# One layer of a gMLP / RG-LRU / HGRN2 encoder on one core: branch generators cut into smaller steps, gate sigmoids moved to the merge phase, one bank emptied by ScalarE

## The chip, the cores and the metric

The kernel runs on one NeuronCore of a Trainium2 chip. Its engines are TensorE (PE; its weight loads are shown apart as PEld), VectorE (DVE), ScalarE (ACT), GpSimd (POOL) and SyncE (SP, used for DMA issue). The time is device microseconds of one execution. The kernel before takes 2251.32 us (median of 3 runs, 2247.9 to 2254.17).

## What is computed

One inference step of one layer for two request groups side by side, 512 new frames and 32 streaming frames (T = 544 columns), D = 2048:

```python
h  = rmsnorm(x, norm_g) * (1.0 + scale) + shift          # scale, shift, gate from silu(c) @ w_ada
z  = h @ w_in                                            # 2048 x 15360, 120 blocks of 128 columns
au, av, ag, lx, lg, hq, hf, hi, hg, mg = split(z)        # 8 blocks each, mg 48 blocks
ya = gelu(au) * (tril(ws) @ rmsnorm(gelu(av)) + bs) * silu(ag)              # gMLP
yb = rglru(causal_conv(lx)) * silu(lg)                                      # RG-LRU, a scan over time
yc = rmsnorm(hgrn2(silu(hq), hf, hi)) * onorm_g * silu(hg)                  # 8 heads, chunks of 64
ga, gb, gc = split(sigmoid(mg), 3)
out = (ga * (ya @ wb0) + gb * (yb @ wb1) + gc * (yc @ wb2)) @ w_out
y = rmsnorm(x + gate * out, final_g)
```

All is float32, with new states of the RG-LRU and HGRN2 branches as further outputs.

## The kernel before

Activations lie transposed: 128 features on the partitions, the 544 frames as columns, taken as two halves of HF = 272. Every large product is done with three matmuls per 128x128 weight tile: weights and activations are split into a rounded high part and a rest (`wh`, `wl`), and hi·hi, hi·lo and lo·hi are added in PSUM (`rows3`). ScalarE makes `wh` by a Copy, VectorE makes `wl` by a subtraction (`split`, called by `halved`, two tiles of 512 columns per weight half).

The first phase makes scale and shift. The second, the z phase, makes z = h @ w_in in 60 `Group`s of two 128-column blocks. A group is a 2x2 block product by a Strassen-like scheme with 7 products (numbers 1 to 7), each 8 weight tiles x 3 = 24 matmuls of 272 columns. Each product is an *item*: `prep` (the splits, and for products 7 and 6 a VectorE addition of two weight halves), `mul` (the 24 matmuls) and `after` (emptying of the PSUM bank). The order over groups is 2, 6, 1 of the next group, 5, 7 of the next group, 3, 4. Four banks (`pm`) are shared: products 1, 6, 5 and 3 add up in bank `a`, which ScalarE copies out after 1, 6, 5 and 3; product 2 has the bank `a2`, which the *next* group uses as its `a`, so that product 1 of the next group, two items later, needs it empty. VectorE empties bank `a2` at line 381 (it adds `u1`, the copy of product 1), and bank `c` at lines 390 and 395.

What is to be done with a group's two outputs stands in generators: `av_gen` and `gm_gen` (gMLP), `hg_gen` (one HGRN2 head), `lru_gen` (one block of the RG-LRU); `keep` post-processes and stores the outputs that are read later, in DRAM scratch. `pump()` advances every started generator by one step, up to its next `yield`; it is called once after each item. The head generators run one at a time, and every third call of `pump` leaves them out (`heads["tick"]`).

Nothing reorders the work: each engine executes its instructions in the order in which the Python code calls them. The main loop does, for item i: weight loads, `prep` of item i+2, `mul` of item i, `after` of item i, `pump`. So what a generator step calls on ScalarE stands between the emptying of bank i and the splits of item i+3. Adding DMAs (`load_adds`, line 266) are issued from GpSimd's queue.

The groups stand in `z_groups`: 4 of av, then 16 times a head group (hf/hq or hi/hg) and a *light* one (two blocks of mg), 3 light ones, 16 heavy ones (8 gMLP, 8 RG-LRU) with a light one after every fourth, and the rest of the light ones.

The third phase (`merge`) multiplies each branch output with its weight matrix in 48 blocks of 48 matmuls and scales each block by its gate, read back from scratch (`fetch`); the last (`out_items`) multiplies with w_out and normalizes.

Of the kernel before, what the change touches and what calls it, by code (L numbers as in the profile page):

```python
# [10 lines left out]
AF = mybir.ActivationFunctionType  # L11
# [95 lines left out]
def hybrid_step_kernel(ctx: ExitStack, tc: tile.TileContext, xT, cT, w_first, w_in, w_branch, w_out,  # L107
# [222 lines left out]
    class Group:  # L330
# [4 lines left out]
        def __init__(self, n, b1, b2, post, posts=None):  # L335
            self.n, self.b, self.post, self.posts = n, (b1, b2), post, posts or {}
            self.w, self.raw = {}, {}
# [4 lines left out]
        def add(self, i):  # L342
# [8 lines left out]
            elif i in (6, 4):  # L351
                n = self.q
            else:
                n = need({1: w_half(b1, 0), 2: w_half(b1, 1), 3: w_half(b2, 1), 5: w_half(b1, 0)}[i])
                if i == 5:
                    add(k - 5, n, w_half(b2, 0))
                else:
                    self.raw[i] = n

            def prep():  # L360
                assert not any(e[1] == n for e in adds)
                self.w[i] = halved(raws[n])
                if i in (7, 6):
                    m = self.raw[1 if i == 7 else 2]
                    tt(raws[n], raws[n], raws[m], op=OP.add)  # L365
                    done[m] = True
                elif i not in (1, 2):
                    done[n] = True

# [4 lines left out]
            def after():  # L374
# [76 lines left out]
    heads = {"next": 0, "ready": 0, "run": None, "tick": 0}  # L451

    def pump():
# [3 lines left out]
        heads["tick"] += 1  # L457
        if heads["tick"] % 3 == 0:
            return
# [169 lines left out]
    def av_gen(j, b):  # L629
        yield  # L630
# [29 lines left out]
    def gm_gen(g, cell):  # L660
# [23 lines left out]
        u, sg = cell["o"]  # L684
        a, s = px(), px()
# [44 lines left out]
    def hg_gen(h):  # L730
# [12 lines left out]
        t1, t2, g = hbuf(), hbuf(), zf  # L743
        act(t1.ap, zf.ap, AF.Abs)
        act(t2.ap, zf.ap, AF.Relu)
        ts(g.ap, zf.ap, 0.0, None, op0=OP.min)
        KO = qb.col - kb.col
# [734 lines left out]
```

## Time and profile before

| | |
|---|---|
| median of 3 runs | 2251.32 us |
| the profiled execution: its time, its span | 2244.99 us, 2243.3 us |
| PE busy in the span | 2052.4 us (91%) |
| DVE, ACT, POOL busy | 1292.6, 1138.4, 511.5 us (58%, 51%, 23%) |
| mean granted clock of PE | 0.953 |

The profile is one execution, taken by the hardware profiler. Times are us from the start of the span unless marked ns. "L381" is line 381 of the kernel; a line can be that of a helper (L190 is the call of every ScalarE activation, L232 the subtraction of every split, L324 every matmul of `rows3`). Names are the program's tile names: `pm` and `pp` are PSUM banks of the z phase and of the later phases, `px` small PSUM tiles of the generators, `arena` the pool of all SBUF buffers of the generators, `raw` and `q` loaded weights. In "x <- y" after a wait, y is the engine and line that ended it. PEclk is the granted share of TensorE's full clock: 1.00 is 2.4 GHz, 0.50 is 1.2 GHz.

### The profile page before, as it was taken

The numbers are of one execution on the slowest core, as the hardware profiler recorded it, in microseconds if no ns is written. First come the engines' busy times: TensorE is split into PE (matmuls) and PEld (weight loads), VectorE is DVE, ScalarE is ACT, GpSimd is POOL, SyncE is SP. The second block draws the span as 40 slices with busy tenths as digits, with TensorE's granted clock in tenths as the row PEclk, the third lists the DMA queues.
The fourth block names the chain that finished last, engine by engine and source line by source line (L and its number), as shares of the span: only waits on it lengthen the run. The fifth ranks groups of instructions, "written<-read, shape, count | busy, mean of one in ns | idle before, by whom it ended". The sixth has DMA issues, their size and how long they took to land.

```text
span 2243.3 us, 40766 instructions
## 1 busy us (share of the span) xinstructions
PE 2052.4 (91%) x15864; PEld 1944.7 (87%) x15864; DVE 1292.6 (58%) x2204; ACT 1138.4 (51%) x2163; POOL 511.5 (23%) x720
## 2 busy tenths in 40 slices
PE   5789979898999899899999999889998999999997
PEld 3279979898988888899899999888987999999996
DVE  3465557666656566557576676777775433442226
ACT  3456545656455566556565655466564322332223
POOL 0011123222223222323233132121122222220112
PEclk8689989999999989999999999999999999999998
DMA  7966656565556656566667776656665677665554
GB/s 308 365 189 181 191 150 192 157 183 166 146 165 165 176 156 185 144 171 174 175 187 202 174 209 175 166 144 166 154 164 187 221 197 184 195 199 182 172 170 165
DMA packets 135010, 412.23 MB, mean 184 GB/s; under 512 B 16128, under 2 KB 38432, under 8 KB 134816
## 3 DMA queue, kind: packets, MB, share of 16 engines
q1 hardware_dynamic: 87408, 261.08, 34.9%
q0 software_dynamic: 41424, 138.34, 27.0%
q10 hardware_dynamic: 5984, 10.19, 1.4%
q8 instruction: 125, 2.05, 0.4%
q14 instruction: 69, 0.57, 0.1%
HBM read 363.77 MB, written 45.78 MB: 183 GB/s over the span
## 4 chain that ended last, share of the span: by engine, by line
PE 55%; DVE 6%; issue 4%; ACT 3%; DMA 1%; POOL 1%; DVEq 0%; ACTq 0%; POOLq 0%
PE pm L324 29%; PE pp L324 22%; DVE wl L232 2%; ACT arena L190 1%; PE px L1067 1%; DVE q L365 1%; PE px L1263 1%; ACT wh L190 1%; PE px L814 1%; DVE arena L1052 0%; ACT L194 0%; DVE arena L381 0%; POOL arena L751 0%; DVE arena L395 0%; ACT L190 0%
## 5 line engine op out<-in xcount | busy, mean ns | idle before, releaser
L324 PE MATMUL pm<-x,wh 128*128 128x272 f32 x6720 | 1315.9, 295 | 76.3 <-DVE arena L381 29.8
L324 PEld LDWEIGHTS pm<-x,wh 128*128 128x128 f32 x6720 | 1087.2, 194 | 87.7 <-ACT wh L190 34.9
L324 PE MATMUL pm<-x,wl 128*128 128x272 f32 x3360 | 988.0, 294 | 5.2 <-DVE wl L232 4.8
L324 PEld LDWEIGHTS pm<-x,wl 128*128 128x128 f32 x3360 | 648.5, 193 | 9.5 <-DVE wl L232 9.4
L232 DVE TENSOR_TENSOR wl<-raw,wh 128x512 fp32r<-128x512 f32 x652 | 466.4, 742 | 303.1 <-ACT wh L190 301.9
L190 ACT ACTIVATE wh<-raw 128x512 fp32r<-128x512 f32 x652 | 387.9, 624 | 326.8 <-PE pp L324 174.8
L324 PE MATMUL pp<-x,wh 128*128 128x272 f32 x2560 | 485.9, 289 | 0.6 <-DVE arena L395 0.6
L324 PEld LDWEIGHTS pp<-x,wh 128*128 128x128 f32 x2560 | 401.2, 189 | 14.9 <-issue 14.3
L324 PE MATMUL pp<-x,wl 128*128 128x272 f32 x1280 | 369.0, 288 | 0.0
L232 DVE TENSOR_TENSOR wl<-q,wh 128x512 fp32r<-128x512 f32 x360 | 252.5, 721 | 199.4 <-ACT wh L190 196.9
L190 ACT ACTIVATE wh<-q 128x512 fp32r<-128x512 f32 x360 | 218.0, 624 | 121.2 <-PE pm L324 94.5
L190 ACT ACTIVATE arena<-arena 128x544 f32<-128x544 f32 (+5 forms) x310 | 160.7, 554 | 195.4 <-DVE arena L1316 76.8
L324 PEld LDWEIGHTS pp<-x,wl 128*128 128x128 f32 x1280 | 240.8, 188 | 0.2 <-DVE wl L232 0.2
L190 ACT ACTIVATE arena<-pm 128x272 f32<-128x272 f32 x240 | 94.0, 392 | 163.4 <-PE pm L324 143.1
L266 POOL DMA_DIRECT2D q<-in_w_in_dram x60 | 54.9, 915 | 483.8 <-DMA q<-in_w_in_dram 120.1
L365 DVE TENSOR_TENSOR q<-q,raw 128x1024 f32<-128x1024 f32 x120 | 148.5, 1238 | 4.1
L190 ACT ACT_TABLE_LOAD x72 | 92.4, 1283 | 54.8 <-DVE arena L1052 49.5
L266 POOL DMA_DIRECT2D raw<-in_w_in_dram x60 | 54.1, 902 | 213.5 <-DMA raw<-in_w_in_dram 89.6
L788 POOL TENSOR_TENSOR arena<-arena 128x544 f32<-128x544 f32 (+1 forms) x40 | 53.5, 1359 | 57.1 <-PE px L816 30.0
L1219 DVE TENSOR_TENSOR arena<-pp,arena 128x544 f32<-128x544 f32 x48 | 34.8, 724 | 41.8 <-PE pp L324 41.8
L190 ACT ACTIVATE arena<-px 128x128 f32<-128x128 f32 (+4 forms) x136 | 43.1, 332 | 24.6 <-PE px L897 13.8
L1326 POOL TENSOR_TENSOR tail<-tail,arena 128x544 f32<-128x544 f32 (+1 forms) x15 | 18.6, 1241 | 150.3 <-ACT arena L190 150.3
(265 smaller groups left out, 1467.1 us busy)
## 6 DMA issues: line engine op xcount, KB each, us to landing
raw<-in_w_in_dram SPq DMA_DIRECT2D x240, 512.0 KB, 4.9
q<-in_w_in_dram SPq DMA_DIRECT2D x60, 512.0 KB, 4.9
q<-in_w_in_dram POOLq DMA_DIRECT2D x60, 512.0 KB, 7.2
raw<-in_w_in_dram POOLq DMA_DIRECT2D x60, 512.0 KB, 6.5
raw<-in_w_branch_dram SPq DMA_DIRECT2D x48, 512.0 KB, 4.2
raw<-in_w_ss_dram SPq DMA_DIRECT2D x44, 512.0 KB, 7.1
raw<-in_w_out_dram SPq DMA_DIRECT2D x38, 512.0 KB, 4.7
raw<-in_w_gate_dram SPq DMA_DIRECT2D x32, 512.0 KB, 4.6
```

The source lines that it names most:

```text
L190: return nc.scalar.activation(out, in_, func, **kw)
L232: tt(lo, src, hi.bitcast(F32), op=OP.subtract)
L266: nc.gpsimd.dma_start(out=raws[n], in_=src, accum_op=OP.add)
L324: mm(p, a, rhs(k, r), start=start and i == 0 and q == 0, stop=stop and i == n - 1 and q == 2, **kw)
L365: tt(raws[n], raws[n], raws[m], op=OP.add)
L788: ptt(v, fv(src, 0, [[2 * m, nb], [m - 1, 2], [1, m]]), fv(src, m - 1, [[2 * m, nb], [0, 2], [0, m]]), op=OP.subtract)
L814: mm(fv(p, 64 * i, [[128, 2], [1, 64]]), x[:, 256 * i + 128:256 * i + 256], fv(x, 256 * i, [[256 + m, 2], [2 * m, nb], [1, m]]), start=Tru ...
L1067: mm(ri[n][h], w.ap[:, n * 128:(n + 1) * 128], xc.ap[:, h * HF:(h + 1) * HF], start=True, stop=True)
L1219: tt(two(g.ap), halves(p), two(g.ap), op=OP.mult)
L1263: mm(p[32 * i:32 * i + 2, :256], cs[:, 4 * q + i, :], w[:, i * 256:(i + 1) * 256], start=q == 0, stop=q == 3)
L1326: ptt(a[:, n], a[:, n], b.ap[:, n], op=OP.add)
```

## The change

Work that a generator did in one step is cut by further `yield`s, mostly so that a step has work of one kind of engine. `pump` advances the head generator at every call instead of two of three. The sigmoids of hq and hg become a generator of their own (`put_away`); the sigmoid of mg is left out there, and made in the merge phase on the gate that was read back. Bank `a2` is emptied by ScalarE, and `u1` is added later, in SBUF, with product 4. One light group more stands ahead of the heavy ones, and so one less after them. The rewriting of `prep` leaves its order as it was.

```diff
@@ class Group: after
                 elif i == 2:
                     self.o1 = buf()
-                    tt(self.o1.ap[:, :HF], banks[self.a2], self.u1.ap, op=OP.add)
-                    self.u1.free()
+                    act(self.o1.ap[:, :HF], banks[self.a2], AF.Copy)
...
                 elif i == 4:
+                    tt(self.o1.ap[:, :HF], self.o1.ap[:, :HF], self.u1.ap, op=OP.add)
                     tt(self.o1.ap[:, HF:], c, self.u2.ap, op=OP.add)
+                    self.u1.free()
@@ pump
-        heads["tick"] += 1
-        if heads["tick"] % 3 == 0:
-            return
@@ av_post, av_gen
-                act(o.ap, o.ap, AF.Gelu_apprx_tanh)
                 start(av_gen(j + i, o))
...
     def av_gen(j, b):
+        yield
+        act(b.ap, b.ap, AF.Gelu_apprx_tanh)
         yield
@@ gm_gen
         act(t1.ap, sg.ap, AF.Sigmoid)
+        yield
         tt(sg.ap, sg.ap, t1.ap, op=OP.mult)
         tt(sg.ap, sg.ap, u.ap, op=OP.mult)
+        yield
@@ hg_gen (28 yields in place of 18)
         act(t1.ap, t1.ap, AF.Exp, scale=-1.0)
         act(t1.ap, t1.ap, AF.Ln, bias=cv[:, 1:2])
+        yield
+        ts(g.ap, zf.ap, 0.0, None, op0=OP.min)
         ptt(g.ap, g.ap, t1.ap, op=OP.subtract)
         tt(t2.ap, t2.ap, t1.ap, op=OP.add)
+        yield
         act(kb.ap, t2.ap, AF.Exp, scale=-1.0, bias=ln1)
         ts(t1.ap, g.ap, -80.0, None, op0=OP.max)
+        yield
         act(t1.ap, t1.ap, AF.Exp, scale=-1.0)
         act(t1.ap, t1.ap, AF.Ln, scale=lb, bias=l1)
...
         lev_e(16)
         lev_e(8)
+        yield
         lev_w(16)
         lev_w(8)
         yield
         p1, p2 = lev_mm(16), lev_mm(8)
+        lev_d(4)
+        lev_d(2)
         yield
         lev_put(16, p1)
         lev_put(8, p2)
-        lev_d(4)
-        lev_d(2)
         lev_e(4)
         lev_e(2)
+        yield
         lev_w(4)
         lev_w(2)
@@ lru_gen (11 yields in place of 8)
         xs.free()
+        yield
         act(x.ap, sg.ap, AF.Sigmoid)
+        yield
         tt(sg.ap, sg.ap, x.ap, op=OP.mult)
         x.free()
-        yield
         ri = [[px()[:, :HF] for _ in range(2)] for _ in range(2)]
@@ z_groups: put_away in place of the body of keep's post
+        def put_away(n, o, on=None):
+            if n[:2] in ("hq", "hg"):
+                yield
+                t = buf()
+                act(t.ap, o.ap, AF.Sigmoid)
+                yield
+                if n[:2] == "hq":
+                    tt(o.ap, o.ap, t.ap, op=OP.mult)
...
+            nc.gpsimd.dma_start(out=spill(n), in_=o.ap)
...
-                    if n[:2] == "mg":
-                        act(o.ap, o.ap, AF.Sigmoid)
...
-        todo += light[16:19]
-        rest = iter(light[19:])
+        todo += light[16:20]
+        rest = iter(light[20:])
@@ merge, pre(j)
                 fetch(j + 1)
+                act(got["g", j].ap, got["g", j].ap, AF.Sigmoid)
```

How the instructions move is seen first on ScalarE, in the z phase, where a head generator makes the logarithm of the forget gate (`cv` and `lbt` are small constants that its Ln and Exp read). Before:

```order
L190 ACTIVATE arena<-pm_116 128x272
L190 ACTIVATE arena<-arena 128x544 x2
L194 ACT_TABLE_LOAD
L190 ACTIVATE arena<-arena 128x544
L190 ACTIVATE arena<-arena,cv 128x544
L190 ACTIVATE arena<-arena,lbt 128x544
L190 ACTIVATE arena<-arena 128x544
L190 ACTIVATE arena<-arena,lbt 128x544
L190 ACTIVATE wh<-q 128x512 x2
```

The same work of the same head in the changed kernel:

```order
L190 ACTIVATE arena<-arena 128x544 x2
L194 ACT_TABLE_LOAD
L190 ACTIVATE arena<-arena 128x544
L190 ACTIVATE arena<-arena,cv 128x544
L190 ACTIVATE wh<-q 128x512 x2
L190 ACTIVATE wh<-raw 128x512 x2
L190 ACTIVATE arena<-pm_116 128x272
L190 ACTIVATE arena<-arena,lbt 128x544
L190 ACTIVATE wh<-raw 128x512 x2
L190 ACTIVATE arena<-pm_115 128x272
L190 ACTIVATE arena<-arena 128x544
L190 ACTIVATE arena<-arena,lbt 128x544
```

Splits of weights (`wh`) and copies of banks (`pm`) now stand between the parts of the chain.

The second place is VectorE in a gMLP group, from product 4 of one group to product 2 of the next. Before:

```order
L395 TENSOR_TENSOR arena<-pm_117,arena 128x272
L692 TENSOR_TENSOR arena<-arena 128x544
L693 TENSOR_TENSOR arena<-arena 128x544
L695 SCALAR_TENSOR_TENSOR arena<-px,par,arena 128x512
L697 SCALAR_TENSOR_TENSOR arena<-px,par,arena 128x32
L232 TENSOR_TENSOR wl<-raw,wh 128x512 x2
L381 TENSOR_TENSOR arena<-pm_115,arena 128x272
L701 TENSOR_TENSOR arena<-arena 128x544
```

In the changed kernel, where L397 and L398 belong to product 4, L696 to L702 to the generator:

```order
L397 TENSOR_TENSOR arena<-arena 128x272
L398 TENSOR_TENSOR arena<-pm_117,arena 128x272
L232 TENSOR_TENSOR wl<-raw,wh 128x512 x4
L696 TENSOR_TENSOR arena<-arena 128x544
L697 TENSOR_TENSOR arena<-arena 128x544
L232 TENSOR_TENSOR wl<-q,wh 128x512 x2
L370 TENSOR_TENSOR q<-q,raw 128x1024
L700 SCALAR_TENSOR_TENSOR arena<-px,par,arena 128x512
L702 SCALAR_TENSOR_TENSOR arena<-px,par,arena 128x32
```

The emptying of bank `a2` (L381) has left VectorE, the generator's four operations stand in two places with splits between them, and the addition from SBUF (L397) has come in.

## Rows read from the trace of the kernel before

**Rows 1.** Busy time by stretch: start:end, us, PE PEld DVE ACT POOL, PEclk, DMA, GB/s.

```profile
150.00:1725.00 1575.00, 1449.88 (x11018) 1404.85 (x11017) 1021.28 (x1717) 929.78 (x1783) 399.93 (x591) 0.96 0.63 171
1200.00:1400.00 200.00, 195.60 (x1536) 192.98 (x1536) 137.60 (x214) 113.94 (x189) 52.18 (x83) 1.00 0.72 190
306.80:317.00 10.20, 4.17 (x18) 4.20 (x19) 5.70 (x13) 3.93 (x9) 0.65 (x2) 0.50 0.34 107
429.70:439.90 10.20, 5.17 (x22) 5.03 (x23) 5.78 (x9) 5.75 (x11) 4.04 (x4) 0.50 0.24 71
```

**Rows 2.** Waits of PE from 150 to 1725 us: total us, times, longest us.

```profile
PE pm L324 <- DVE arena L381: 29.8, 16, 10.8
PE pm L324 <- ACT arena L190: 25.7, 9, 7.3
PE px L814 <- DVE arena L803: 17.5, 6, 5.9
PE px L1067 <- DVE arena L1052: 13.9, 5, 2.8
PE pm L324 <- ACT wh L190: 13.7, 5, 4.6
PE px L1067 <- issue: 8.4, 2, 5.6
PE px L878 <- DVE arena L868: 7.1, 3, 2.8
```

**Rows 3.** PE in time: start, us, what, [idle before <- releaser].

```profile
312.83 0.79 PE L324 MATMUL pm<-x,wh 128*128 128x272 f32 x2 [10.85 <-DVE arena L381]
...
1267.99 0.49 PE L324 MATMUL pm<-x,wh 128*128 128x272 f32 x2 [0.64 <-DVE arena L381]
...
1698.96 0.52 PE L324 MATMUL pm<-x,wh 128*128 128x272 f32 x2 [2.18 <-ACT arena L190]
1709.53 0.82 PE L324 MATMUL pm<-x,wh 128*128 128x272 f32 x2 [5.77 <-ACT arena L190]
```

**Rows 4.** ACT in time, one head's chain, 653 to 664 us.

```profile
653.56 1.21 ACT L190 ACTIVATE arena<-arena 128x544 f32<-128x544 f32 x2 [1.65 <-DVE arena L390]
654.79 1.28 ACT L194 ACT_TABLE_LOAD   x1
656.08 0.66 ACT L190 ACTIVATE arena<-arena 128x544 f32<-128x544 f32 x1
656.77 0.75 ACT L190 ACTIVATE arena<-arena,cv 128x544 f32<-128x544 f32 x1
658.31 0.75 ACT L190 ACTIVATE arena<-arena,lbt 128x544 f32<-128x544 f32 x1 [0.79 <-DVE arena L752]
659.98 0.66 ACT L190 ACTIVATE arena<-arena 128x544 f32<-128x544 f32 x1 [0.92 <-DVE arena L754]
661.41 1.13 ACT L190 ACTIVATE wh<-q 128x512 fp32r<-128x512 f32 x2
```

**Rows 5.** Groups by line and shape, 150 to 1725 us: busy us, mean ns | idle before.

```profile
L381 DVE TENSOR_TENSOR arena<-pm,arena 128x272 f32<-128x272 f32 x59 | 25.6, 434 | 1.6 <-PE pm L324 1.6
...
L190 ACT ACTIVATE arena<-pm 128x272 f32<-128x272 f32 x237 | 92.8, 392 | 161.5 <-PE pm L324 141.2 <-DVE arena L381 10.3 <-DMA d_hf<-arena 5.4
L190 ACT ACT_TABLE_LOAD x71 | 91.1, 1283 | 53.0 <-DVE arena L1052 49.5 <-DVE arena L395 2.4
```

**Rows 6.** Waits of ACT and POOL, whole span: total us, times, longest us.

```profile
ACT wh L190 <- PE pp L324: 174.8, 84, 3.1
...
POOL q L266 <- DMA q<-in_w_in_dram: 120.1, 20, 13.7
...
ACT arena L190 <- POOL arena L788: 6.1, 4, 4.1
```

**Rows 7.** DMA issues: count, KB each, median us from issue to landing.

```profile
arena<-d_mg POOLq DMA_DIRECT2D x32, 272.0 KB, 4.4
```

**Rows 8.** The chain that ended last, a merge block: start, us, what.

```profile
1988.51 6.21 PE pp L324 x48
```

More of the change, by code (lines that the diff above doesn't have):

```diff
@@ L336, in __init__ @@
             self.n, self.b, self.post, self.posts = n, (b1, b2), post, posts or {}
-            self.w, self.raw = {}, {}
+            self.w, self.raw, self.seen = {}, {}, set()
             self.a, self.a2, self.c = n % 2, (n + 1) % 2, 2 + n % 2
@@ L354, in add @@
                 n = need({1: w_half(b1, 0), 2: w_half(b1, 1), 3: w_half(b2, 1), 5: w_half(b1, 0)}[i])
+                self.raw[i] = n
                 if i == 5:
                     add(k - 5, n, w_half(b2, 0))
-                else:
-                    self.raw[i] = n
             def prep():
@@ L362, in prep @@
                 self.w[i] = halved(raws[n])
[L363 to L367, printed above, removed]
-                    done[n] = True
+                self.seen.add(i)
+                if i in (3, 4, 5):
+                    done[n] = True
+                else:
+                    m = {1: 7, 7: 1, 2: 6, 6: 2}[i]
+                    if m in self.seen:
+                        r = self.raw[min(i, m)]
+                        tt(raws[self.q], raws[self.q], raws[r], op=OP.add)
+                        done[r] = True
             def mul():
@@ L448, in start @@
         bg.append(gen)
-    heads = {"next": 0, "ready": 0, "run": None, "tick": 0}
+    heads = {"next": 0, "ready": 0, "run": None}
     def pump():
@@ L831, in hg_gen @@
         yield
+        act(fv(g64.ap, 0, [[64, 9], [1, 32]]), fv(g32.ap, 0, [[64, 9], [1, 32]]), AF.Copy)
+        ptt(fv(g64.ap, 32, [[64, 8], [1, 32]]), fv(g32.ap, 32, [[64, 8], [1, 32]]),
+            fv(g32.ap, 31, [[64, 8], [0, 32]]), op=OP.add)
         lev_e(16)
         lev_e(8)
+        yield
         lev_w(16)
@@ L899, in hg_gen @@
         w32.pop("b").free()
+        pv = px()
+        for w in range(4):
+            nc.tensor.transpose(pv[:, w * 128:(w + 1) * 128], zi.ap[:, w * 128:(w + 1) * 128], ident)
+        yield
         for b, lo, f in ((ke, 0, 128), (qe, 64, 64)):
@@ L904, in hg_gen @@
         vt, kt, vk = hbuf(NP), hbuf(NP), hbuf(256)
-        pv = px()
-        for w in range(4):
-            nc.tensor.transpose(pv[:, w * 128:(w + 1) * 128], zi.ap[:, w * 128:(w + 1) * 128], ident)
         for b in range(2):
@@ L933, in hg_gen @@
         nc.sync.dma_start(out=s0.ap[:, :128], in_=S0[:, h, :])
+        yield
+        act(kt.ap, pk, AF.Copy)
+        act(vk.ap[:NS], pq[:NS, :256], AF.Copy)
+        at = hbuf(256)
+        act(at.ap, pq[:, 256:], AF.Copy)
         yield
@@ L940, in hg_gen @@
         nc.gpsimd.memset(rs_t[:, h % 2, 0], 1.0)
+        kt.free()
+        yield
         S = hbuf(NP)
@@ L971, in hg_gen @@
         ts(m, m, 1.0 / 128, EPS, op0=OP.mult, op1=OP.add)
+        yield
         act(r, m, AF.Ln)
         act(r, r, AF.Exp, scale=-0.5)
+        yield
         newton(r, m, t)
@@ L1059, in lru_gen @@
         xs.free()
+        yield
         act(x.ap, sg.ap, AF.Sigmoid)
+        yield
         tt(sg.ap, sg.ap, x.ap, op=OP.mult)
         x.free()
-        yield
         ri = [[px()[:, :HF] for _ in range(2)] for _ in range(2)]
@@ L1106, in z_groups @@
         av = [(B_AV + j, B_AV + j + 1, av_post(j)) for j in range(0, 8, 2)]
+        def put_away(n, o, on=None):
+            if n[:2] in ("hq", "hg"):
+                yield
+                t = buf()
+                act(t.ap, o.ap, AF.Sigmoid)
+                yield
+                if n[:2] == "hq":
+                    tt(o.ap, o.ap, t.ap, op=OP.mult)
+                else:
+                    stt(o.ap, o.ap, P("onorm_g"), t.ap, op0=OP.mult, op1=OP.mult)
+                t.free()
+            nc.gpsimd.dma_start(out=spill(n), in_=o.ap)
+            o.free()
+            if on:
+                on()
+            yield
         def keep(*names, on=None):
@@ L1111, in post @@
                 for n, o in zip(names, os):
-                    if n[:2] == "mg":
-                        act(o.ap, o.ap, AF.Sigmoid)
-                    elif n[:2] in ("hq", "hg"):
-                        t = buf()
-                        act(t.ap, o.ap, AF.Sigmoid)
-                        if n[:2] == "hq":
-                            tt(o.ap, o.ap, t.ap, op=OP.mult)
-                        else:
-                            stt(o.ap, o.ap, P("onorm_g"), t.ap, op0=OP.mult, op1=OP.mult)
-                        t.free()
-                    nc.gpsimd.dma_start(out=spill(n), in_=o.ap)
-                    o.free()
-                if on:
-                    on()
+                    g = put_away(n, o, on if n == names[-1] else None)
+                    if n[:2] in ("hq", "hg"):
+                        start(g)
+                    else:
+                        next(g)
             return post
```

20 lines of the change are left out of this document (6 added, 14 removed).

## The prediction

> **What bounds the kernel now.** I read the busy time by stretch first. From 150 to 1725 us, the z phase, PE is busy for 1449.9 of 1575.0 us: it stands still for 125.1 us. Its mean granted clock there is 0.96, while between 1200 and 1400 us, where the gMLP groups run, it is 1.00 and PE is busy for 97.8% [rows 1]. There 1536 matmuls take 195.6 us, 127.3 ns each, so an item of 24 matmuls lasts 3.06 us. At that pace the 11018 matmuls of the phase would need 1403 us; they take 1449.9, so running at the low clock costs about 47 us. The rows at 306.8 and 429.7 show how: in both stretches the clock is at 1.2 GHz after PE had waited, and 18 and 22 matmuls take 4.17 and 5.17 us, 233 ns each [rows 1]. So 125 us of waiting and 47 us of slow running are all that can be won in this phase. DVE (1021 us) and ACT (930 us) are not full; PE waits for their order, not for their throughput.
>
> Then the waits of PE. They fall into few kinds [rows 2]. Bank `a2` not emptied by VectorE: 29.8 us. A bank not emptied by ScalarE: 25.7. A generator's small matmul whose operand VectorE has not written: L814 17.5 and L878 7.1 in the head, L1067 in the RG-LRU 13.9, with 8.4 more that the view puts down to nothing but are the same matmul. A split not made: 13.7.
>
> Last, ScalarE around one of these waits [rows 4]. From 653.56 on it works through one head's chain: two activations, a table load, Exp, Ln, a wait of 0.79 us for VectorE, Exp, a wait of 0.92 us for VectorE, two more. Only at 661.41 does it get to the splits of the next product, 7.9 us after it began. Two items are 6.1 us, so PE runs dry. This is the kernel's trouble in one picture: the step is longer than the two items by which the splits run ahead.
>
> **The change part by part.** *Smaller steps.* An emptying has to be over one item after the one that it empties. Between the end of product i-1 and the point where bank i must be empty lie two items, 6.1 us, and in them ScalarE has the step of i-1, two splits (1.13 us [rows 4]) and the copy (0.392 us [rows 5]); so a step of up to 4.5 us costs nothing. I added up every step's ScalarE work in both orders with the durations of [rows 4, 5]. Before, 12 steps of the z phase are above 4.4 us, by 19 us together, and the waits for other engines inside a step come on top; in the changed kernel 3 are, by 3.0 us together, and a step seldom holds work of two engines that wait for each other. So I let these waits go: 25.7 - 2.18 - 5.77 = 17.7 us for ScalarE's banks (the two that stay are at the end of the phase, where ScalarE waits for reloaded data [rows 3]), and 13.7 us for the splits.
>
> *One more item between a generator's operand and its matmul.* In the head, `lev_e` and `lev_w` were one step with the matmul in the next; now each has its own. In the RG-LRU one more step stands between the convolution and the matmul (L1067). The longest of these waits are 5.9 us in the head, where the activations now run an item earlier than the products that PE needs, and 5.6 us in the RG-LRU, behind its set-up, with 2.8 us as the rule there [rows 2]; 3.06 us more covers all but a part of two. I take all: 17.5 + 7.1 + 13.9 + 8.4 = 46.9 us.
>
> *Bank `a2` by ScalarE.* One of the 16 waits is 10.85 us long, at 312.83 [rows 3]: VectorE sits in the head's set-up, waiting for a DMA of constants, which the change leaves as it is; behind it the splits are late too, whoever empties the bank. The others, 29.8 - 10.8 = 19.0 us, come from the copy standing behind the generator's VectorE work, 0.64 us in every gMLP group (the row at 1267.99). With the bank on ScalarE, and the generator's four operations in two steps, they go. The price is 60 copies of 0.392 us, 23.5 us of ScalarE [rows 5]; the 60 VectorE operations of 0.434 us stay as additions from SBUF, which the trace of before does not show in this size. Between nothing and twice 0.434 us each, I take 0.434, the nearest row. They lie beside PE, as bank `c` is not needed again until two groups later; without that cover they would cost 26 us.
>
> A page speaks against this edit. The Trainium skill, "ScalarE: Activation LUTs", section "Rules for kernel authors", gives additions and the like to VectorE and keeps ScalarE for functions that only it has. By that rule 23.5 us more on ScalarE and nothing less on VectorE is a loss. The trace agrees that nothing is saved in work (392 against 434 ns), but at 930 us of 1575 ScalarE has the room, so the sum stands.
>
> *Gate sigmoids in the merge phase.* 48 activations of 0.66 us leave the z phase, and the table loads in the program fall from 104 to 78, 26 x 1.283 = 33 us of ScalarE; all of this lay beside PE except where a step was too long, which is counted above. In the merge phase each sigmoid waits for its gate, and two splits are queued behind it on ScalarE. The gate is asked for one block ahead, 6.2 us [rows 8], and lands 4.4 us after issue [rows 7]; the splits behind it are for the second block after, and ScalarE already waits 174.8 us there for PE [rows 6]. I take nothing. Without this cover each block would pay up to the landing, 48 x 4.4 = 211 us; that needs the landing to be later by some 10 us.
>
> *Head at every call, one light group moved.* A head takes 29 calls of `pump` (28 yields) where it took 19 steps at two of three calls, 28.5 items; heads become ready every 28 items. The pace is the same; nothing.
>
> **The sum.** Waits that go: 17.7 + 13.7 + 46.9 + 19.0 = 97.3 us of 125.1. The low clock goes in the same share: 47 x 97.3 / 125.1 = 37 us. What comes new: the best stretch of before, 1200 to 1400, still loses 4.4 us in 200, 2.5 of it in four of the 0.64 us waits; the remaining 1% over 1450 us is 14 us, and the three long steps 3.0 us more; with their share of slow running (0.38 us per us of waiting) 23 us. 97.3 + 37 - 23 = 111 us. From the profiled execution, 2245.0, that is 2134. It lay 6.3 us below the median of the three runs, so against these I forecast 2140.
>
> **Rivals.** *The waits move to the next in line.* Each wait that goes has a second behind it: heads now step at every item, so a bank, a split and a small matmul come closer together. For it: three different engines appear as releasers in [rows 2], so no single queue is at fault. Against it: in the gMLP stretch, where steps are small, nothing else is late. If half of the gain comes back: 2251 - 55 = 2196.
>
> A rule would bring about the same. The trace has a table load of 1.28 us with the next activation 0.01 us behind it [rows 4]. The Trainium skill, "ScalarE: Activation LUTs", section "What ACT_TABLE_LOAD costs", adds a drain of about 1.38 us to every switch. Then 23 steps of the changed kernel, not 3, would be above 4.4 us, by 40 us, and with the clock the sum would lose some 51 us, an estimate that ends near 2191. By the row, the drain is not there; I give it 2 in 100, within this rival.
>
> *GpSimd's queue becomes the brake (slower).* ScalarE's Exp in a head waits for GpSimd's subtraction of the step before (L788), three times per head, 24 times. That step was 1.5 items back on average; now it is one. GpSimd issues the adding DMAs in the same queue and stops for the loaded weights: 20 times, 6.0 us each on average, 13.7 at most [rows 6]. A subtraction behind such a stop comes late, ScalarE stands, and with it all splits. At 6.0 us each, with the clock, 24 x 6.0 x 1.38 = 199 us are lost against 111 won: 2251 - 111 + 199 = 2339. It decides from 111 / (24 x 1.38) = 3.4 us per wait. Against it: before, ScalarE lost only 6.1 us to L788 in all [rows 6].
>
> *It doesn't do what it says.* If the waits are set by the splits' two items of lead and not by the steps, only the 0.64 us waits go, and the time stays within a few us: 2246.
>
> **How the numbers follow.** Forecast 0.72; waits move on 0.16; no effect 0.04; slower 0.08. Less than 0.3% (7 us) cannot be told from no change by a measurement of this kernel. The forecast's own range is 2111 (no new waits at all: 97 + 37 + the 6 us that the end of the phase might give) to 2168 (a quarter of the gain comes back). The range that holds 8 in 10 goes on into the first rival, to its middle: 2111 to 2196. Faster: 0.72 + 0.16 = 0.88; the same 0.04; slower 0.08.
>
> **What would show it.** Right: PE idle between 150 us and the end of the z phase falls from 125 to some 45 us, the z phase ends near 1610 us, the clock in it is 0.98 or more; waits of L814's, L878's and L1067's successors are gone; the 10.8 us wait of the set-up and some 8 us at the end of the phase stay. The merge phase lasts as long as before. Wrong: waits of PE for ScalarE's banks above 25 us, ScalarE waiting for GpSimd above 40 us, or idle PE in the merge phase behind the gate sigmoids.

## The result, and the profile after

| | before | after |
|---|---|---|
| median (us) | 2249.61 (2247.8 to 2254.17, 4 runs) | 2212.4 (2209.14 to 2219.2, 4 runs) |
| profiled execution, its span (us) | 2244.99, 2243.3 | 2211.79, 2210.1 |
| granted clock, mean of the span | 0.953 | 0.957 |

The ratio is 0.9836, 95% interval 0.9807 to 0.9864: 37 us faster, and outside the range given. The forecast had a gain of 111 us, so the direction was right and two thirds of the gain are missing. Lines have moved: L390, L395, L788, L803, L814, L868, L878, L1052, L1058 and L1067 of before are now L392, L398, L793, L808, L819, L879, L889, L1067, L1073 and L1083. L381 has no successor on VectorE: its bank is emptied on L190 now, and its addition is L397.

First the busy time by stretch, with the columns of [rows 1]. The z phase now ends at 1680 us (1718 before); both windows run a little beyond its end.

```profile
150.00:1690.00 1540.00, 1441.74 (x11037) 1404.30 (x11036) 1008.70 (x1712) 881.67 (x1766) 389.02 (x586) 0.96 0.64 175
1200.00:1400.00 200.00, 197.56 (x1545) 195.37 (x1544) 134.78 (x219) 113.74 (x195) 54.61 (x86) 0.99 0.72 193
```

PE stands still for 1540 - 1441.7 = 98.3 us, against 125.1 before and some 45 forecast. The slow running shrank too: 1441.74 us for 11037 matmuls is 130.6 ns each; at the 127.3 ns of the gMLP stretch of before they would need 1405 us, so 37 us are lost where it was 47. Together 37 us; the two profiled spans differ by 33, mainly because the start of the merge phase is 5 us longer (below). In the gMLP stretch itself PE is now busy for 98.8%, as forecast.

Next PE's waits from 150 to 1690 us, with the columns of [rows 2].

```profile
PE px L819 <- DVE arena L808: 18.8, 10, 5.1
PE pm L324 <- ACT arena L190: 17.7, 10, 6.1
PE px L889 <- DVE arena L879: 17.3, 7, 5.8
PE pm L324 <- ACT wh L190: 14.9, 4, 8.1
PE px L819 <- ACT wh L190: 12.9, 3, 8.2
...
PE px L1007 <- DVE arena L992: 4.7, 2, 2.7
PE pm L324 <- DVE arena L392: 2.2, 1, 2.2
```

Set beside [rows 2], two kinds went: the bank `a2` behind VectorE (29.8 us; the 2.2 us of L392 are another bank, `c`) and the RG-LRU's matmul (22.3 to 0.6 us, seen in the whole span as the next row). ScalarE's banks fell only from 25.7 to 17.7 us, and the splits rose from 13.7 to 14.9. The head's small matmuls had 24.6 us of waiting, L814 and L878; their successors have twice that, 18.8 + 17.3 + 12.9 = 49.0 us.

```profile
PE px L1083 <- DVE arena L1073: 0.6, 2, 0.3
```

A wait that [rows 2] and [rows 6] gave no place to has grown. These are the largest rows of the whole span in which an engine waits for a *store* that still reads a buffer; of all such rows the sum is 85.9 us, against 21.0 before (d_hf, d_mg and the like in DRAM take what one phase hands to the next).

```profile
ACT arena L190 <- DMA d_mg<-arena: 26.4, 6, 7.3
ACT L190 <- DMA d_hf<-arena: 9.6, 2, 7.6
POOL arena L793 <- DMA d_mg<-arena: 9.4, 2, 5.2
ACT arena L190 <- DMA d_y<-arena: 7.7, 3, 2.8
...
POOL arena L793 <- DMA d_hf<-arena: 5.6, 1, 5.6
```

**One place where an operand stands behind a split**: three engines in time around 590 us, in one head's set-up (columns as in [rows 3] and [rows 4]). ScalarE:

```profile
587.22 1.23 ACT L190 ACTIVATE arena<-arena 128x544 f32<-128x544 f32 x1
588.47 1.28 ACT L194 ACT_TABLE_LOAD   x1
589.76 1.82 ACT L190 ACTIVATE arena<-arena 128x256 f32<-128x256 f32 x4
591.49 1.14 ACT L190 ACTIVATE wh<-raw 128x512 fp32r<-128x512 f32 x2
```

VectorE:

```profile
592.14 2.11 DVE L232 TENSOR_TENSOR wl<-raw,wh 128x512 fp32r<-128x512 f32 x2 [1.78 <-ACT wh L190]
594.17 0.42 DVE L392 TENSOR_TENSOR arena<-arena,pm 128x272 f32<-128x272 f32 x1
594.52 0.68 DVE L808 TENSOR_TENSOR arena<-arena 128x512 f32<-128x512 f32 x1
595.12 0.71 DVE L879 TENSOR_TENSOR arena<-arena 128x544 f32<-128x544 f32 x1
```

TensorE, the matmul that needs the last of these:

```profile
595.89 0.22 PE L889 MATMUL px<-arena 128*32 128x1 f32 x2 [2.35 <-DVE arena L879]
```

ScalarE's step takes from 587.22 to 591.49, 4.3 us, within the 4.5 that were said to cost nothing, and no bank is late. But the split for a product two items ahead is made behind it; VectorE stands 1.78 us for that `wh`, and the multiplication of L879, whose operands ScalarE has left by 591.6, is queued on VectorE behind the `wl` that needs it. TensorE stands still for 2.35 us in front of two matmuls of 0.22 us.

**One place where a buffer is still being stored**, around 1010 us in another head. GpSimd, which issues the store at 1006.38 and then has to write into the buffer that it reads:

```profile
1006.38 0.58 POOL L1138 DMA_DIRECT2D d_hf<-arena  x1
...
1014.67 1.15 POOL L793 TENSOR_TENSOR arena<-arena 128x544 f32<-128x544 f32 x1 [5.62 <-DMA d_hf<-arena]
```

ScalarE, whose Exp needs that result and has the next splits behind it:

```profile
1015.85 0.75 ACT L190 ACTIVATE arena<-arena 128x272 f32<-128x272 f32 x2 [5.38 <-POOL arena L793]
1016.50 1.13 ACT L190 ACTIVATE wh<-raw 128x512 fp32r<-128x512 f32 x2
```

VectorE, which waits for that split and writes the small matmul's operand (L808) only behind it:

```profile
1017.15 1.29 DVE L232 TENSOR_TENSOR wl<-raw,wh 128x512 fp32r<-128x512 f32 x2 [7.55 <-ACT wh L190]
...
1019.00 1.35 DVE L808 TENSOR_TENSOR arena<-arena 128x544 f32<-128x544 f32 x2
```

TensorE, whose L819 reads what L808 writes (the view names ScalarE's `wh`, which ended just before):

```profile
1019.86 1.19 PE L819 MATMUL px<-arena 128*128 128x128 f32 x4 [8.16 <-ACT wh L190]
```

The view of DMA issues gives such stores some 6 us (count, KB each, median us from issue to landing):

```profile
d_mg<-arena POOLq DMA_DIRECT2D x48, 272.0 KB, 6.4
d_hf<-arena POOLq DMA_DIRECT2D x8, 272.0 KB, 6.0
```

Here the one store cost 5.62 us on GpSimd, 5.38 on ScalarE, 7.55 on VectorE and 8.16 on TensorE. Nothing in the program's text asks for that wait: the buffer had been freed, and the arena gave the same place out again.

Two theories came from this. **A, stores:** a freed buffer is taken again while its store runs; ScalarE and GpSimd stop there, and the splits behind them are late. **B, distance:** a small matmul comes one item after its VectorE operand, too near when a split stands between. Against both stands the rival of the prediction, *the waits move to the next in line*, by which taking away one only brings up another.

### The profile page after: what moved, and what is told of

The parts are those of the page before. It is cut to its first block, busy times and chain, and to the rows that moved or that the text cites. A ratio compares the mean times of both kernels' runs of the same rounds, so it can differ in the third digit from the quotient of the medians.

```text
span 2210.1 us, 40668 instructions
## 1 busy us (share of the span) xinstructions
PE 2039.8 (92%) x15864; PEld 1939.4 (88%) x15864; DVE 1284.9 (58%) x2204; ACT 1118.6 (51%) x2197; POOL 503.7 (23%) x720
## 4 chain that ended last, share of the span: by engine, by line
PE 54%; DMA 6%; DVE 5%; issue 5%; ACT 4%; POOL 1%; DVEq 0%; ACTq 0%; POOLq 0%
PE pm L324 29%; PE pp L324 21%; DVE wl L232 2%; ACT arena L190 2%; DMA q<-in_w_in_dram 2%; ACT wh L190 2%; DMA d_mg<-arena 1%; PE px L1290 1%; PE px L819 1%; DMA d_hf<-arena 1%; DMA d_y<-arena 1%; DMA arena<-d_hf 1%; POOL arena L793 0%; DMA arena<-d_y 0%; ACT L190 0%
## 5 line engine op out<-in xcount | busy, mean ns | idle before, releaser
L324 PE MATMUL pm<-x,wh 128*128 128x272 f32 x6720 | 1314.8, 295 | 42.5 <-ACT wh L190 22.6
L324 PEld LDWEIGHTS pm<-x,wh 128*128 128x128 f32 x6720 | 1087.2, 194 | 51.3 <-ACT wh L190 23.8
L324 PE MATMUL pm<-x,wl 128*128 128x272 f32 x3360 | 987.4, 294 | 6.1 <-DVE wl L232 6.0
L232 DVE TENSOR_TENSOR wl<-raw,wh 128x512 fp32r<-128x512 f32 x652 | 458.8, 735 | 406.2 <-ACT wh L190 405.3
L324 PEld LDWEIGHTS pm<-x,wl 128*128 128x128 f32 x3360 | 648.3, 193 | 9.5 <-DVE wl L232 9.3
L190 ACT ACTIVATE wh<-raw 128x512 fp32r<-128x512 f32 x652 | 389.8, 624 | 295.6 <-PE pm L324 197.8
L324 PE MATMUL pp<-x,wh 128*128 128x272 f32 x2560 | 486.2, 289 | 6.1 <-DVE arena L1246 4.5
L324 PEld LDWEIGHTS pp<-x,wh 128*128 128x128 f32 x2560 | 400.9, 188 | 20.9 <-issue 13.5
L232 DVE TENSOR_TENSOR wl<-q,wh 128x512 fp32r<-128x512 f32 x360 | 257.9, 744 | 210.9 <-ACT wh L190 206.8
L324 PE MATMUL pp<-x,wl 128*128 128x272 f32 x1280 | 368.7, 288 | 0.0
L190 ACT ACTIVATE wh<-q 128x512 fp32r<-128x512 f32 x360 | 214.8, 625 | 126.5 <-PE pm L324 90.9
L190 ACT ACTIVATE arena<-arena 128x544 f32<-128x544 f32 (+5 forms) x310 | 162.8, 554 | 198.7 <-DVE arena L1343 76.7
L324 PEld LDWEIGHTS pp<-x,wl 128*128 128x128 f32 x1280 | 240.6, 188 | 0.2 <-DVE wl L232 0.2
L190 ACT ACTIVATE arena<-pm 128x272 f32<-128x272 f32 x300 | 117.1, 390 | 222.6 <-PE pm L324 153.2
L793 POOL TENSOR_TENSOR arena<-arena 128x544 f32<-128x544 f32 (+1 forms) x40 | 51.5, 1301 | 49.6 <-PE px L821 18.8
L819 PE MATMUL px<-arena 128*128 128x128 f32 x160 | 30.9, 321 | 31.7 <-DVE arena L808 18.8
L1246 DVE TENSOR_TENSOR arena<-pp,arena 128x544 f32<-128x544 f32 x48 | 34.7, 723 | 39.4 <-PE pp L324 39.4
L819 PEld LDWEIGHTS px<-arena 128*128 128x128 f32 x160 | 24.1, 213 | 34.6 <-ACT wh L190 16.2
```

What stands on the lines that cost most here:

```text
L190: return nc.scalar.activation(out, in_, func, **kw)
L232: tt(lo, src, hi.bitcast(F32), op=OP.subtract)
L324: mm(p, a, rhs(k, r), start=start and i == 0 and q == 0, stop=stop and i == n - 1 and q == 2, **kw)
L793: ptt(v, fv(src, 0, [[2 * m, nb], [m - 1, 2], [1, m]]), fv(src, m - 1, [[2 * m, nb], [0, 2], [0, m]]), op=OP.subtract)
L819: mm(fv(p, 64 * i, [[128, 2], [1, 64]]), x[:, 256 * i + 128:256 * i + 256], fv(x, 256 * i, [[256 + m, 2], [2 * m, nb], [1, m]]), start=Tru ...
L1246: tt(two(g.ap), halves(p), two(g.ap), op=OP.mult)
```

## The experiments

All are timed against the kernel before; "below after" and "above after" set their medians beside 2212.4. To tell places apart, the span of the profiled execution is cut at the same products by number, the 51st, 286th and 358th of the 420 of the z phase: the heads, the gMLP groups, and the RG-LRU to the end of the z phase. In the kernels read here every head has ended before the 286th. For before these are 931.5, 242.2 and 251.5 us; for after 918.6, 233.1 and 239.4. What is left apart hardly moves: the stretch ahead of the heads (168.3 to 164.5), the merge phase but its first four blocks (266.6 and 266.7) and the output (234.6 in both).

**Stored buffers rest for four items.** The kernel after, in which the arena does not hand out a buffer that was stored until four calls of `pump` later, if another fits.

```diff
     def find(self, m):
-        b = self.busy
+        b = [x or u > Arena.tick for x, u in zip(self.busy, self.until)]
+        k = self.fit(m, b)
+        return self.fit(m, self.busy) if k is None else k
...
     nc.gpsimd.dma_start(out=spill(n), in_=o.ap)
-    o.free()
+    o.free(True)
```

`free(True)` sets `until` to `Arena.tick` + 4, and `pump` counts the ticks; the same stands at every other buffer that is stored.

> The changed kernel, with one difference: an SBUF buffer that was just stored to DRAM is not handed out again for four calls of pump, as long as another is free. Theory A (buffers are reused while their store still reads them, so ScalarE and GpSimd stop in front of the splits): the waits for such stores, 86 us over ACT, POOL and DVE in the trace of the changed kernel, fall below 15 us, PE's waits in the z phase fall by 20 us or more, and the time is 2175 to 2190 us. Theory B (VectorE makes a small matmul's operand behind splits that are late for another reason): the waits for stores go, but PE's waits at the small matmuls L819 and L889, 49 us, stay above 35 us, and the time is 2200 to 2212 us.

Measured: 2185.18, ratio 0.972 (0.9686 to 0.9754), 27 us below after. The store waits of the span fall from 85.9 to 2.6 us. The waits of B stay, and those for ScalarE's banks and splits fall (PE's waits, 150 to 1725 us; L828, L898 and L332 are L819, L889 and L324 there):

```profile
PE px L828 <- DVE arena L817: 21.3, 9, 4.3
PE px L898 <- DVE arena L888: 14.4, 6, 3.8
PE pm L332 <- ACT arena L198: 11.0, 4, 6.6
PE pm L332 <- ACT wh L198: 10.6, 4, 4.9
```

A holds, for about 27 us; 14.5 of them in the heads (918.6 to 904.1) and 9.5 in the RG-LRU's stretch.

**The heads' steps as before.** The kernel after with the head's generator and its two steps in three items as they were: `lev_e` and `lev_w` in one step, the chain of the set-up in one.

```diff
+        heads["tick"] += 1
+        if heads["tick"] % 3 == 0:
+            return
...
         act(t1.ap, t1.ap, AF.Ln, bias=cv[:, 1:2])
-        yield
         ts(g.ap, zf.ap, 0.0, None, op0=OP.min)
...
         lev_e(8)
-        yield
         lev_w(16)
```

> The changed kernel with the head generator of before, steps and two-of-three calls of pump included; all else as changed. Theory (the head's smaller steps won next to nothing): 2205 to 2225 us, with PE waiting 60 us or more in the head stretch, as in both kernels. Rival, the step of the prediction that the head's smaller steps are worth their 50 us of waits and 20 us of clock: 2255 us or more.

Measured: 2205.86, ratio 0.9817 (0.9785 to 0.985), at the low end of what was expected; against after the intervals overlap. The heads' stretch is 920.0 us with the old steps and 918.6 with the new. The 6.5 us between the medians are no more than the noise, and the stretches put them where no head runs (RG-LRU 231.2 us, 239.4 in after). So the most laborious part of the change won nothing here: the waits of PE only have other names (150 to 1725 us; L822 and L886 are L819 and L889 there):

```profile
PE pm L324 <- ACT arena L190: 42.9, 20, 7.8
PE px L886 <- DVE arena L876: 11.8, 5, 3.9
PE px L822 <- DVE arena L811: 11.4, 7, 2.5
...
PE px L822 <- ACT arena L190: 3.5, 3, 2.2
```

The banks wait 42.9 us where the new steps leave 17.7; the small matmuls wait 26.7 where the new have 49.0. Not shown is what the new steps would win with the stores out of the way: in the heads' stretch after has 68.1 us of store waits and this kernel 42.4, and resting buffers were not tried with the old steps.

**The bank alone.** The kernel before, with only bank `a2` emptied by ScalarE and the product added in SBUF.

```diff
-                    tt(self.o1.ap[:, :HF], banks[self.a2], self.u1.ap, op=OP.add)
-                    self.u1.free()
+                    act(self.o1.ap[:, :HF], banks[self.a2], AF.Copy)
...
+                    tt(self.o1.ap[:, :HF], self.o1.ap[:, :HF], self.u1.ap, op=OP.add)
+                    self.u1.free()
```

> The kernel before with one part of the change alone: bank a2 emptied by ScalarE, the first product added in SBUF with product 4. By the prediction's sum 19 us of waits and 7 us of clock go: 2224 us. Rival (in the head stretch the bank was late because ScalarE was, and only the eight 0.64 us waits of the gMLP stretch and a few more go): 2238 to 2250 us, with new waits of PE for ScalarE's banks in place of those for VectorE's.

Measured: 2235.21, ratio 0.994 (0.9924 to 0.9957): some 14 us, half of what the sum expected and between its time and the rival's. Without smaller steps most of the wait only changes queues: the 29.8 + 25.7 us of the two rows of banks in [rows 2] become one row of 43.8. This kernel also has 51.1 us of store waits against 21.0, so a part of what keeps ScalarE's queue late may be stores:

```profile
PE pm L324 <- ACT arena L190: 43.8, 16, 10.0
```

**One more item in front of the small matmuls.** The kernel after with one more step before `lev_mm(16)` and before `lev_mm(1)`; two steps elsewhere are joined, so that a head takes as many items as it did. The load of `zi` is asked one step earlier with it.

```diff
         lev_w(8)
         yield
+        yield
         p1, p2 = lev_mm(16), lev_mm(8)
...
+        zi = hbuf()
+        nc.gpsimd.dma_start(out=zi.ap, in_=scratch[f"hi {h}"])
+        yield
         p1 = lev_mm(1)
...
         lev_put(1, p1)
-        yield
...
-        yield
         act(r, m, AF.Ln)
```

> The changed kernel with one more call of pump between the VectorE operands and the small matmuls at two places of the head (levels 16 and 8; level 1 with the key product, the place of L889), and two later steps joined so that a head takes as many calls as in the changed kernel. Theory B (operand behind late splits, one item is too short): the waits at L889's place, 17 us, and those at the first of the two L819 places go, and the time is 2180 to 2195 us. Theory A (only reused buffers matter): the waits turn up one item later, at splits and banks, and the time is 2206 to 2218 us.

Measured: 2168.48, ratio 0.9634 (0.9594 to 0.9673), 44 us below after and more than B expected. The heads take 884.1 us (918.6). The successors of L814 and L878 wait 7.9 us in all, and the joined steps bring 13.5 us at another matmul, 4.7 in after (PE's waits, 150 to 1725 us):

```profile
PE px L1007 <- DVE arena L992: 13.5, 6, 3.9
PE px L819 <- DVE arena L808: 4.5, 5, 1.9
PE px L819 <- ACT wh L190: 3.4, 2, 2.4
```

B is shown: the same instructions, only one item further apart. But not all of the 44 us is B's. 34.5 lie in the heads' stretch; 8.4 lie in the RG-LRU's (239.4 to 231.0), where no head runs. The store waits fell as well, from 85.9 to 49.4 us, since the buffers' order changed, and in the RG-LRU's stretch they went from 12.5 to nothing: these 8.4 us are most likely A's.

**Both.** The two edits above together.

> The changed kernel with both differences at once: stored buffers held back for four calls of pump, and one more call between operand and small matmul at two places of the head. If the two causes are separate, the gains add: 2212 - 27 - 44 = 2141 us, 2135 to 2150. If both cure the same waits, it ends near the better of the two, 2158 to 2168 us.

Measured: 2149.85, ratio 0.9543 (0.9526 to 0.956). The two alone gave 27.2 and 43.9 us; together they give 62.5 of 71.1. They are two causes that overlap by some 9 us, and the stretches show where: in the heads' the two take 14.5 and 34.5 us alone and 50.9 together (918.6 to 867.7), in the RG-LRU's 9.5 and 8.4 alone and 10.9 together. With the stores out of the way one more item is worth 35 us (2185.18 to 2149.85). That is the price of B.

**The RG-LRU's steps as before.** The kernel after with the RG-LRU's generator as it was.

```diff
         xs.free()
-        yield
         act(x.ap, sg.ap, AF.Sigmoid)
-        yield
         tt(sg.ap, sg.ap, x.ap, op=OP.mult)
         x.free()
+        yield
         ri = [[px()[:, :HF] for _ in range(2)] for _ in range(2)]
```

(and its later steps likewise)

> The changed kernel with the RG-LRU generator of before, its three fewer steps included; all else as changed. Theory (the RG-LRU part of the prediction held, 22 us of waits and some 10 us of clock): 2237 to 2248 us, with waits of some 2.8 us at each of the eight block products again. Rival (those waits would have gone anyway, since the gate sigmoids and one light group left that stretch): below 2225 us.

Measured: 2224.89, ratio 0.9884 (0.9864 to 0.9905): the new steps are worth some 12 us, not the 30 of theory; the interval touches that of after, so the 12 are rough. The time falls just inside the rival's range, but the rival's reason does not hold: the wait of before's L1067 comes back with the old steps, 14.7 + 5.7 us (PE's waits, 150 to 1725 us). In its own stretch the old steps cost 15.4 us (239.4 to 254.8). After had got other waits there: resting the stored buffers took 9.5 us more off it.

```profile
PE px L1082 <- DVE arena L1067: 14.7, 5, 3.5
PE px L1082 <- DVE arena L1071: 5.7, 1, 5.7
```

**The gates' sigmoids back in the z phase.** The kernel after, with the sigmoid before the store, none in the merge phase.

```diff
+            if n[:2] == "mg":
+                act(o.ap, o.ap, AF.Sigmoid)
             nc.gpsimd.dma_start(out=spill(n), in_=o.ap)
...
-                act(got["g", j].ap, got["g", j].ap, AF.Sigmoid)
```

> The changed kernel with the sigmoids of mg made in the z phase again, before the store, and not in the merge phase. Theory (moving them is worth little in the z phase, and costs the merge phase the 5 us that it got longer): 2204 to 2214 us, the merge phase and the rest 525 us as before. Rival (48 activations and their table loads would lengthen ScalarE's steps in the z phase): 2222 us or more.

Measured: 2225.92, ratio 0.9893 (0.9851 to 0.9935), 13.5 us above after; the intervals overlap a little, so that number is rough. The heads' stretch is where it is paid: 939.9 us instead of 918.6, while the first four blocks of the merge phase get back 4.1 us (29.2 to 25.1). The table loads on one line rise from 57 to 72 in the z phase (columns as in [rows 5]). In after, 150 to 1690 us:

```profile
L190 ACT ACT_TABLE_LOAD x57 | 73.1, 1283 | 17.3 <-DMA d_hf<-arena 9.6 <-DMA arena<-d_mg 4.4 <-DVE arena L1067 2.4
```

In this kernel, 150 to 1725 us:

```profile
L190 ACT ACT_TABLE_LOAD x72 | 92.4, 1283 | 11.9 <-DMA d_hf<-arena 8.3 <-DVE arena L1067 2.4
```

**A version that goes on.** Both edits, with the joined step elsewhere, so that L1007 gets its item back.

```diff
         kt.free()
-        yield
         S = hbuf(NP)
...
         ts(m, m, 1.0 / 128, EPS, op0=OP.mult, op1=OP.add)
+        yield
         act(r, m, AF.Ln)
```

> As e5_both, but the two later steps that are joined to keep the number of calls are other ones: the state's products and their VectorE use, in place of the squares and the Ln behind them, whose joining gave 13.5 us of waits at L1007. If that wait was the price of the joining, it goes: 8 to 15 us below e5_both. If it only moves to the state's step: within 5 us of e5_both.

Measured: 2145.37, ratio 0.9523 (0.9507 to 0.954): 4.5 us below the kernel with both, which the intervals don't separate. L1007's successor (L1016) falls from 13.6 to 5.9 us. The z phase is now near what was forecast for the change itself (150 to 1625 us):

```profile
150.00:1625.00 1475.00, 1419.68 (x11054) 1383.37 (x11052) 1012.39 (x1716) 885.06 (x1772) 397.90 (x586) 0.98 0.66 183
```

PE stands still for 55.3 us, and at 128.4 ns a matmul loses 12 us to the low clock.

**Resting buffers in the kernel before.**

> The kernel before with the holding back of stored buffers alone. Its trace shows 21 us of waits for stores over ACT, POOL and DVE, against 86 in the changed kernel. Theory (the reuse of buffers under a store was a small matter before, and the change made it one that counts): 2240 to 2250 us, a quarter of the 27 us that the same edit took off the changed kernel, or less. Rival (it was as costly before, hidden in waits put down to other engines): 2222 to 2232 us.

Measured: 2249.75, ratio 0.9998 (0.9979 to 1.0016). Before, the reuse cost nothing that can be told from the noise (some 4 us); it is a cost that the change brought in. The number of stored buffers that are taken again within four items hardly differs (34 in the program before, 38 in the one after): it is where they fall that changed.

**The gates' sigmoids as a step of their own.** The kernel of "a version that goes on", the sigmoid of a gate run in the middle of the block instead of ahead of the next splits.

```diff
+        def gate(g):
+            act(g.ap, g.ap, AF.Sigmoid)
+            yield
...
-                act(got["g", j].ap, got["g", j].ap, AF.Sigmoid)
+                start(gate(got["g", j]))
```

> As e8_best, with the gate's sigmoid of each merge block called in the middle of the block, behind the splits of the second block after, and not ahead of them. If the longer start of the merge phase (four blocks of 29 us in place of 24) comes from splits behind the sigmoid that waits for its gate: 4 to 6 us less, 2139 to 2142 us. If it comes from the RG-LRU's last steps, which now reach into that phase: within 2 us of e8_best.

Measured: 2144.63, ratio 0.9531 (0.9499 to 0.9562), the same as without. The first four merge blocks take 28.1 us (29.6 without the edit, 24.1 before). That the sigmoids stand ahead of the splits is thus not shown to be the whole cause; the last steps of the RG-LRU reach into these blocks too. Two kernels above bear on it: with no sigmoid in the merge phase the four blocks take 25.1 us, with the RG-LRU's old steps 26.5, where after has 29.2. So both have a part, and the shares stay open. It is 4 to 5 us in all.

## Why the prediction was wrong, step by step

**"One more item between a generator's operand and its matmul": failed, the largest part of the miss.** I took all 46.9 us of L814, L878 and L1067. In the heads the change did not put an item more between operand and matmul: it moved `lev_e` an item earlier but left `lev_w`, which writes the operand, one step ahead of `lev_mm`; and since heads step at every item, the skipped ones, which had given half of these matmuls a second item, are gone. The order of the instructions in the traces shows it. A head has three such places (levels 16 and 8, levels 4 and 2, level 1 with the key product), so eight heads have 24; each cell gives how many, and PE's waits there together:

| | operand one item ahead | operand two items ahead |
|---|---|---|
| before | 12 places, 17.1 us | 12 places, 7.4 us |
| after | 24 places, 49.1 us | none |
| after, with the heads' steps as before | 12 places, 22.8 us | 12 places, 3.9 us |
| after, with one more item | 8 places, 7.9 us | 16 places, 0.0 us |

The term forecast 24.6 us won; 24.4 were lost. I had compared the waits with the 3.06 us of an item and not asked what stands on VectorE in front of the operand: a `wl` that waits for ScalarE. One item really more is worth some 35 us. In the RG-LRU the wait did go (22.3 to 0.6 us), but the stretch became only 12.1 us shorter, as stores took some of it: with stored buffers resting it is 21.6 us shorter (251.5 to 229.9). The mechanism was right there, and a part of the gain was spent on a wait that I had not counted.

**"Smaller steps": the rule of 4.5 us holds for banks and splits, and I used it as if nothing else mattered.** The rows at 587.22 show a step of 4.3 us that no bank noticed and a small matmul did. Of the 31.4 us that I let go (17.7 of banks, 13.7 of splits) little came: the two rows of PE's waits still have 17.7 and 14.9 us, 8.0 less of banks and 1.2 more of splits. With the old steps the heads take 920.0 us, with the new 918.6. Stores hid a part of what the steps won: with stored buffers resting the two rows have 11.0 and 10.6 us. One reading was wrong as well: of the two waits at the end of the phase that were to stay, the one of 2.18 us went; before it ScalarE had stood 2.57 us for VectorE's L395, not for reloaded data.

**A term that was missing: stores.** I listed what each engine waits for and left out that a freed buffer can still be read. Before there were 21.0 us of such waits, none with a price; after 85.9, with a price of 27 us. One row had warned: in [rows 5] ScalarE's copies had stood still 5.4 us for the store `d_hf<-arena`, and I passed over it. The same rest in the kernel before changed nothing (ratio 0.9998), so the price came in with the new order.

**"Bank `a2` by ScalarE": right in kind, somewhat too large.** The 29.8 us behind VectorE are gone. The 19.0 us with their share of the clock would be 26; the bank alone gave some 14, because ScalarE's queue made the bank late instead. The addition from SBUF, for which I had no row and took 0.434 us, takes 439 ns on L397 (60 of them, 26.3 us). The rule of the Trainium skill that I set against the edit ("ScalarE: Activation LUTs", "Rules for kernel authors") names `relu`, `max`, `min`, `add` and `mul` for VectorE; the addition has stayed there, and what moved is a plain copy, so the rule says less against the edit than I made of it. The loss did not come: the 296 copies from banks in the z phase, the new ones among them, took 390 ns each, and the edit by itself is faster.

```profile
L190 ACT ACTIVATE arena<-pm 128x272 f32<-128x272 f32 x296 | 115.5, 390 | 219.5 <-PE pm L324 150.2 <-DVE arena L1073 30.2 <-DMA d_mg<-arena 22.7
```

**"Gate sigmoids in the merge phase: I take nothing": wrong to the better.** Moving them is worth some 13 us, all of it in the heads' stretch, where with the sigmoids back PE waits longer for ScalarE's banks (26.3 us, 17.7 in after) and at L889 (24.8, 17.3 in after); the price at the start of the merge phase, some 4 us, is in that already. The merge phase was to last as long as before; its first four blocks are 5.1 us longer (24.1 to 29.2), the others are not.

**"Head at every call, one light group moved: nothing".** Neither was run by itself. With the old steps and the old stepping together the heads' stretch is the same, and so the pace is as said; but the stepping at every call is what put all 24 places at one item, and to that I gave no price.

**The low clock.** The share rule (0.38 us of slow running per us of waiting) held: waits 125.1 to 98.3, slow running 47 to 37. In the version that goes on it is 55.3 and 12, 0.22 per us, so it is no fixed share.

**The sum, in place of 111 us:** bank some 14, gates 13.5, RG-LRU 12, each measured by itself, and the heads' steps nothing or up to 7 us lost: 33 to 40, against 37 measured. The smaller steps of the gMLP generators and the moved light group were not run by themselves; the gMLP stretch is 9.1 us shorter, of which the bank alone takes 3.2. Single edits overlap, so this is a balance and not a proof.

**The rivals.** *The waits move to the next in line* (2196) came nearest, and went past its own price: the waits in the two rows of banks fell by 37.8 us, and those of the heads' small matmuls rose by 24.4. The reason given for it, steps of heads at every item, is the right place. The drain behind every table load that went with it (the Trainium skill, "ScalarE: Activation LUTs", "What ACT_TABLE_LOAD costs") stays unseen: the load at 588.47 ends at 589.75, and the next activation starts at 589.76. *GpSimd's queue becomes the brake*: ScalarE waited 20.8 us for L793, 15 times, where 24 waits of 3.4 us would decide. That is above the 6.1 us of [rows 6], and a part of it is stores, as at 1014.67.

```profile
ACT arena L190 <- POOL arena L793: 20.8, 15, 5.4
```

*It doesn't do what it says* fell: three parts show their price one by one. Of the three signs that were to show it wrong, two did not come: ScalarE's banks stayed under 25 us, its waits for GpSimd under 40. The third, idle PE in the merge phase behind the gate sigmoids, came in a small way. At the start of the merge phase ScalarE stands 4.35 us for a gate that is read back; the splits and, behind them on VectorE, the product that empties a bank (L1246) are late, and PE waits for it three times (its waits from 1679 to 1712 us; before has none):

```profile
1685.77 1.28 ACT L190 ACT_TABLE_LOAD   x1 [4.35 <-DMA arena<-d_mg]
```

```profile
PE pp L324 <- DVE arena L1246: 4.5, 3, 2.5
```

The list had neither the stores nor the queue in front of an operand, so it could not have told where the 74 us went. Of the signs of being right, only the waits of L1067 and `a2` went as said: PE stands still for 98 us and not 45, the phase ends at 1680 us and not 1610, and its clock stays at 0.96. What was to stay did stay, but for the 2.18 us above: a set-up wait (8.15 us now, 10.85 before) and one at the end of the phase (6.10 us now, 5.77 before); PE in time:

```profile
312.01 0.82 PE L324 MATMUL pm<-x,wh 128*128 128x272 f32 x2 [8.15 <-ACT wh L190]
...
1670.03 0.82 PE L324 MATMUL pm<-x,wh 128*128 128x272 f32 x2 [6.10 <-ACT arena L190]
```

## What to carry to other kernels

A step's length says whether an engine keeps up with its banks; whether a matmul's operand comes in time depends on what stands ahead of that operand in its own queue, and what *that* waits for. So before a wait is taken as gone, follow the operand's queue back one instruction, and count the items between operand and matmul in the new order, not in the old one plus one. And where buffers come from a common pool, a change of order moves which buffer meets a running store: look at the waits for stores in the new order, and keep stored buffers out of use for longer than a store lasts (here four items, some 12 us, for stores of some 6 us; no other length was tried).

## What the runs showed of the hardware

A store of 272 KB on GpSimd's queue took 3.6 to 6.4 us from issue to landing (medians by target), and an engine that writes into its buffer sooner waited up to 7.6 us; by the queues' order one such wait passed through four engines, 5.62, 5.38, 7.55 and 8.16 us. A PSUM bank of 128x272 emptied by ScalarE took 390 ns, against 434 ns of VectorE's addition from the same shape of bank [rows 5].
